# Raw places of the down projection: every second chunk loaded into another tile

## Chip, cores and metric

The kernel runs on one core of a Trainium2 chip. The metric is the device time of one execution in microseconds; the median of some runs is compared. The core has a matmul engine (PE, with its weight loads as PEld), a vector engine (DVE), an activation engine (ACT), GpSimd (POOL), and SyncE (SP), whose queue issues nearly all the transfers here.

## What is computed

A decoder trunk of two layers on 512 rows of 1024 float32 values. Each layer mixes the rows with two kinds of attention heads and then runs a SwiGLU feed-forward network; each half is normed before and after and added to the input:

```python
h = rms_norm(x, attn_pre_g[l])
proj = h @ w_in[l]                 # differential and forgetting heads, both causal
...
x = x + rms_norm(mixed @ w_out[l], attn_post_g[l])

h = rms_norm(x, ffn_pre_g[l])
y = (jax.nn.silu(h @ w_gate[l]) * (h @ w_up[l])) @ w_down[l]
x = x + rms_norm(y, ffn_post_g[l])
```

The hidden width is 2816, so `w_down` is 2816 x 1024. All is float32. Every weight is split into a rounded high part (type float32r) and the remainder, and each product is made of three matmuls: high x high, high x low, low x high.

## The kernel before

**Down projection.** It is done by Strassen's scheme in the Winograd form: seven products of half-size blocks in place of eight. The hidden vectors are kept as "operands" (tiles op00 to op35, a group of six per block or sum, in the pool hp of the layer), the weights as four raw blocks of `w_down` and four sums of blocks, which `weight_sums` (L1215) forms while the gate and up products run and writes to a DRAM scratch `t_d`. Sums of operands are written to `s_d` and come back through `reload` (L1319).

**Chunks.** `product` (L1313) walks over a block's 11 row tiles in six chunks, five of 256 rows and one of 128. For each chunk `chunk_w` (L1298) calls `load_w` (L247): SP loads the raw chunk, 512 KB, into a raw tile; ACT casts it to the high part wh (L258); DVE subtracts to get the low part wl (L259); then 12 matmuls (6 for the short one) use wh and wl. The raw tile has the tag wr with two buffers; wh and wl have three buffers each. The same three tags serve the gate and up weights and the projections of the attention, in program order. There are 42 chunks in a layer, in seven products in the order of L1334 to L1375: banks A_, C_, A_, B_, A_, B_, A_. The last three chunks of the last product are loaded by one statement (`ws`, L1375), and their matmuls are done for one row block after the other, with the post-norm and the next layer's pre-norm between.

**Other tiles that the change touches.** `gain` (L234) loads a row of norm gains, spread over all partitions, into a tile of the pool gpool with the tag gain and two buffers, and pins the load behind what was traced on SP before it. g_apost and g_fpre are used up before the gate and up products; g_fpost and g_apre (of the next layer) are loaded after the last gate and up product. g_fpost is first read at L1356, g_apre in the pre-norm of the next layer. p5, y0, u3 and y2 (L1349) are partial results that take over the tiles op30 to op33 once product 3, which reads group 3, has used them. VA_TAGS (L39) names the operand tiles that serve as raw, high and low tiles for the value weights of the next layer, which are loaded during the last products.

**Order.** Instructions of one engine run in the order in which the framework's scheduler has put them; a tile is given to its next user when all readers of the former one are done, in program order within a tag. In the down projection only the tail after the `ws` loads is pinned by hand.

Of the kernel before, what the change touches and what calls it, by code (L numbers as in the profile page):

```python
# [11 lines left out]
F32 = mybir.dt.float32  # L12
# [5 lines left out]
P = 128  # L18
S = 512
NT = S // P  # L20
D = 1024
# [3 lines left out]
DEPTH = 2  # L25
# [10 lines left out]
TB = S // 16  # L36
VA_C, VA_T = 4, 1
TAIL = 3
VA_TAGS = (("34", "00", "01"), ("34", "02", "03"), ("14", "10", "11"), ("34", "12", "13"))  # L39
KSPLIT = 4  # L40
EPS = 1e-6
BIG = 1e30
# [132 lines left out]
def hymba_block(ctx, tc, x_d, pos_d, apre_d, win_d, fb_d, lq1_d, lk1_d, lq2_d, lk2_d, dsg_d, wout_d, apost_d,  # L175
# [7 lines left out]
    gpool = ctx.enter_context(tc.tile_pool(name="gpool", bufs=2))  # L183
# [50 lines left out]
    def gain(src, l, name):  # L234
        t = gpool.tile([P, D], F32, name=name, tag="gain")
        tc.keep_in_program_order(nc.sync.dma_start(t, src[l].partition_broadcast(P)))
        return t
# [9 lines left out]
    def load_w(src, shape, name, eng=None, dst=None, raw=None):  # L247
        n = int(np.prod(shape[1:]))

        def t(tag, dt):  # L250
            w = wpool.tile([P, WCH], dt, name=f"{tag}_{name}", tag=tag)[:, :n]
            return w.rearrange("p (a b) -> p a b", a=shape[1])
        if raw is None:
            w = wpool.tile([P, WCH], F32, name=f"wr_{name}", tag="wr", bufs=NRAW)[:, :n]
            raw = w.rearrange("p (a b) -> p a b", a=shape[1])
        hi, lo = dst or (t("wh", F32R), t("wl", F32R))
        nc.sync.dma_start(raw, src)
        A.copy(hi, raw)  # L258
        (eng or V).tensor_sub(lo, raw, hi.bitcast(F32))  # L259
        return hi, lo  # L260
# [86 lines left out]
    for l in range(DEPTH):  # L347
# [849 lines left out]
        with ExitStack() as fctx:  # L1197
            hp = fctx.enter_context(tc.tile_pool(name=f"ffn{l}", bufs=1, reuse_waits="tile"))
# [37 lines left out]
            def swiglu(f, pg, pu):  # L1236
                sg = half_tile(f"sg{l}{f}")
                A.activation(sg, pg, AF.Silu)
                V.tensor_mul(sg, pu, sg)  # L1239
                if f < FH:  # L1240
                    first[f] = sg
                    put(0, f, sg[:, :TH])
                    return
                f -= FH
                a11, a21, a12, a22 = (x[:, c] for x in (first.pop(f), sg) for c in (slice(0, TH), slice(TH, S)))
                put(1, f, a12)
                nc.sync.dma_start(s_d[2, f], a22)
                w = half_tile(f"s12{l}{f}")
                s1, s2 = w[:, :TH], w[:, TH:]
                V.tensor_add(s1, a21, a22)  # L1250
                V.tensor_sub(s2, s1, a11)
                put(3, f, s1)
                put(2, f, s2)
                w = half_tile(f"s34{l}{f}")
                s3, s4 = w[:, :TH], w[:, TH:]
                V.tensor_sub(s3, a11, a21)
                V.tensor_sub(s4, a12, s2)
                nc.sync.dma_start(s_d[0:2, f].rearrange("x p n -> p x n"), w.rearrange("p (x n) -> p x n", x=2))
                weight_sums(f)
# [22 lines left out]
            for f in ORDER[2:]:  # L1282
# [1 line left out]
                g_part()  # L1284
                u_part()
                swiglu(f, pg, pu)
            g_fpost = gain(fpost_d, l, f"g_fpost{l}")
            if l + 1 < DEPTH:
                g_apre = gain(apre_d, l + 1, f"g_apre{l + 1}")

            def side(x):

                if x < 4:
                    return t_d[x]
                z, c = divmod(x - 4, 2)
                return wd[z * FH * P:(z + 1) * FH * P, CH[c]]

            def chunk_w(x, q, dst=None):  # L1298
                n = min(2, FH - 2 * q)
                src = side(x)[2 * q * P:(2 * q + n) * P].rearrange("(k p) n -> p k n", p=P)  # L1300
                return load_w(src, [P, n, S], f"d{l}{x}{q}", dst=dst)

            def product_mm(bank, g, q, w, m):
                a = opd[g, q]
                tk = slice(m * P, (m + 1) * P)
                n = a.shape[1]
                for k in range(n):
                    s, e = q == k == 0, q == QN - 1 and k == n - 1
                    mm(bank, a[:, k, 0, tk], w[0][:, k], s, False)
                    mm(bank, a[:, k, 0, tk], w[1][:, k], False, False)  # L1310
                    mm(bank, a[:, k, 1, tk], w[0][:, k], False, e)

            def product(banks, g, x, qs=None):  # L1313
                for q in qs or range(QN):
                    w = chunk_w(x, q)
                    for m in range(2):
                        product_mm(banks[m], g, q, w, m)
# [11 lines left out]
            QN = (FH + 1) // 2  # L1329
            A_, C_, B_ = ([mk(f"d{x}{l}{m}") for m in range(2)] for x, mk in (("a", bank_t), ("c", bank_s),  # L1330
                                                                             ("b", bank_g)))
            name = f"fp{l}"
# [12 lines left out]
            for m in range(2):  # L1345
                V.tensor_add(u[m], A_[m], u[m])
            reload(1, 1)
            product(B_, 3, 0)
            p5, y, u3, y2 = (hp.tile([P, 2, S], F32, name=f"{x}{l}", tag=f"op3{q}") for q, x in enumerate(  # L1349
                ("p5", "y0", "u3", "y2")))  # L1350
            for m in range(2):
                A.copy(p5[:, m], B_[m])
            reload(2, 2)
            for t in range(2):
                ys[t] = y[:, t]
                V.tensor_mul(ys[t], c11[t], g_fpost[:, CH[0]])  # L1356
            product(A_, 0, 2)
            for m in range(2):
                V.tensor_add(u3[:, m], A_[m], u[m])
                V.tensor_add(u[m], p5[:, m], u[m])  # L1360
# [8 lines left out]
            for m in range(2):  # L1369
# [3 lines left out]
                V.tensor_mul(ys[2 + m], ys[2 + m], g_fpost[:, CH[1]])  # L1373
            product(A_, 2, 3, range(QN - TAIL))
            ws = [chunk_w(3, q) for q in range(QN - TAIL, QN)]  # L1375
            if not last:
                for c in range(4):
                    raw, hi, lo = (hp.tile([P, 2, S], dt, name=f"wv{x}{l}{c}", tag=f"op{tag}") for x, dt, tag in zip(
                        "rhl", (F32, F32R, F32R), VA_TAGS[c]))
                    src = win_d[l + 1][2 * c * P:(2 * c + 2) * P, VA:VA + S].rearrange("(k p) n -> p k n", p=P)  # L1380
# [5 lines left out]
            a = f"a{l + 1}"  # L1386
# [43 lines left out]
```

## Time and profile before

| | us |
|---|---|
| median of 3 runs | 1303.62 (1300.08 to 1303.75) |
| profiled execution, in all | 1306.31 |
| its span, first to last instruction | 1304.5 |
| PE busy | 1227.0 (94%) |
| DVE busy | 818.3 (63%) |
| ACT busy | 600.7 (46%) |
| mean granted PE clock | 0.977 |

The span is a little shorter than the execution's time, and the profiled execution is 2.7 us above the median. A busy PE is not a PE at its peak: a matmul of 512 columns shows about 0.39 us of busy time, though the next one starts sooner. So starts, not durations, tell its pace. The granted clock says what share of full speed the chip allowed the matmul engine in a stretch.

### The profile page before, as it was taken

The page shows a single profiled execution, that of the slowest core. Times are in us where ns is not written, and L with a number is a line of the kernel's source. Part 1 is how long each engine was busy: PE and PEld are TensorE (multiplying, and loading weights), DVE is VectorE, ACT ScalarE, POOL GpSimd, SP SyncE. Part 2 cuts the span into 40 slices and gives each one's busy share as a digit, 9 for nine tenths or more (in the row PEclk, how much of TensorE's full clock was granted, in tenths as well). Part 3 has the DMA queues.
Part 4 walks back from the last instruction along what each step waited for, and adds up shares of the span by engine and source line. Part 5 has one row for each costly group of instructions (what it writes and reads, how often), then busy time and mean ns, then how long its engine had stood idle before and what let it go on. Part 6 is the DMA issues. An engine that isn't in the chain of part 4 may idle for free.

```text
span 1304.5 us, 16741 instructions
## 1 busy us (share of the span) xinstructions
PE 1227.0 (94%) x5817; PEld 998.2 (77%) x5817; DVE 818.3 (63%) x1574; ACT 600.7 (46%) x1162; POOL 209.9 (16%) x250
## 2 busy tenths in 40 slices
PE   8999999999999999898899999989999999998885
PEld 6787877898888888666677778768988888876664
DVE  6697768655464646555739876885555555546555
ACT  5476767443332323443535766764423232325432
POOL 1212457210000000000222224761000000000001
PEclk8999999999999999898999999999999999999997
DMA  7233343317676766776413333441366666667543
GB/s 236 75 95 90 89 131 114 96 50 237 202 224 199 222 202 225 255 223 189 144 34 97 98 98 96 117 143 49 107 208 212 212 213 211 217 227 245 184 151 121
DMA packets 211268, 206.75 MB, mean 158 GB/s; under 512 B 11680, under 2 KB 155680, under 8 KB 211184
## 3 DMA queue, kind: packets, MB, share of 16 engines
q1 hardware_dynamic: 211040, 205.16, 51.1%
q8 instruction: 46, 0.75, 0.2%
q10 hardware_dynamic: 144, 0.52, 0.1%
q14 instruction: 38, 0.31, 0.1%
HBM read 163.34 MB, written 33.91 MB: 151 GB/s over the span
## 4 chain that ended last, share of the span: by engine, by line
PE 42%; issue 34%; DVE 15%; ACT 5%; DMA 3%; POOL 2%; POOLq 0%; DVEq 0%; ACTq 0%; SPq 0%
PE pj_g L205 9%; PE pj_u L205 9%; PE o L205 4%; PE va L205 3%; PE pj_kf L205 2%; DMA wr_d<-in_w_down_dram 2%; PE pj_kd L205 2%; PE db L205 1%; PE dc L205 1%; PE pj_qf L205 1%; PE vb L205 1%; DVE ed L958 1%; DVE ed L875 1%; DVE t2kd L739 1%; PE of L205 1%
## 5 line engine op out<-in xcount | busy, mean ns | idle before, releaser
L259 DVE TENSOR_TENSOR wl_d<-wr_d,wh_d 128x1024 fp32r<-128x1024 f32 x84 | 94.3, 1134 | 97.5 <-ACT wh_d L258 96.8
L258 ACT CAST wh_d<-wr_d 128x1024 fp32r<-128x1024 f32 x84 | 81.9, 977 | 148.4 <-DMA wr_d<-t_d 70.1
L205 PE MATMUL pj_g<-hT_h,wh_g 128*128 128x512 f32 (+1 forms) x384 | 142.9, 372 | 0.0
L205 PE MATMUL pj_g<-hT_h,wl_g 128*128 128x512 f32 (+1 forms) x384 | 142.6, 371 | 0.0
L205 PE MATMUL pj_g<-hT_l,wh_g 128*128 128x512 f32 (+1 forms) x384 | 142.6, 371 | 0.0
L205 PE MATMUL pj_u<-hT_h,wh_u 128*128 128x512 f32 (+1 forms) x368 | 140.1, 381 | 0.0
L205 PE MATMUL pj_u<-hT_l,wh_u 128*128 128x512 f32 (+1 forms) x368 | 139.8, 380 | 0.0
L205 PE MATMUL pj_u<-hT_h,wl_u 128*128 128x512 f32 (+1 forms) x368 | 139.7, 380 | 0.0
L271 POOL TENSOR_SCALAR v_fp<-s_fp 128x1 f32<-128x1 f32 x8 | 4.5, 559 | 741.1 <-ACT junk L277 387.2
L205 PE MATMUL da<-wh_d,op 128*128 128x512 f32 x352 | 116.1, 405 | 6.7 <-ACT wh_d L258 6.7
L258 ACT CAST wh_g<-wr_g 128x1024 fp32r<-128x1024 f32 x44 | 46.3, 1053 | 148.0 <-PE pj_u L205 79.2
L259 DVE TENSOR_TENSOR wl_u<-wr_u,wh_u 128x1024 fp32r<-128x1024 f32 x44 | 53.9, 1225 | 96.0 <-ACT wh_u L258 96.0
L258 ACT CAST wh_u<-wr_u 128x1024 fp32r<-128x1024 f32 x44 | 46.3, 1052 | 132.9 <-PE pj_g L205 125.9
L205 PE MATMUL da<-wl_d,op 128*128 128x512 f32 x176 | 73.8, 419 | 19.9 <-DVE wl_d L259 19.6
L205 PEld LDWEIGHTS da<-wh_d,op 128*128 128x128 f32 x352 | 68.3, 195 | 24.5 <-ACT wh_d L258 10.9
L205 PEld LDWEIGHTS pj_g<-hT_h,wh_g 128*128 128x128 f32 x384 | 72.4, 189 | 12.6
L205 PEld LDWEIGHTS pj_g<-hT_l,wh_g 128*128 128x128 f32 x384 | 72.3, 188 | 12.5
L205 PEld LDWEIGHTS pj_g<-hT_h,wl_g 128*128 128x128 f32 x384 | 72.2, 188 | 12.5
L1239 DVE TENSOR_TENSOR sg<-pj_u,sg 128x512 f32<-128x512 f32 x44 | 30.4, 690 | 81.8 <-PE pj_u L205 81.8
L205 PEld LDWEIGHTS pj_u<-hT_l,wh_u 128*128 128x128 f32 x368 | 69.2, 188 | 13.2
L205 PEld LDWEIGHTS pj_u<-hT_h,wl_u 128*128 128x128 f32 x368 | 69.2, 188 | 13.0
L205 PEld LDWEIGHTS pj_u<-hT_h,wh_u 128*128 128x128 f32 x368 | 69.1, 188 | 13.0
(299 smaller groups left out, 2958.1 us busy)
## 6 DMA issues: line engine op xcount, KB each, us to landing
wr_g<-in_w_gate_dram SPq DMA_DIRECT2D x44, 512.0 KB, 4.3
wr_u<-in_w_up_dram SPq DMA_DIRECT2D x44, 512.0 KB, 4.1
b<-in_w_down_dram SPq DMA_DIRECT2D x88, 256.0 KB, 3.4
t_d<-b SPq DMA_DIRECT2D x88, 256.0 KB, 4.1
wr_d<-t_d SPq DMA_DIRECT2D x40, 512.0 KB, 3.8
wr_d<-in_w_down_dram SPq DMA_DIRECT2D x30, 512.0 KB, 4.5
wr_o<-in_w_out_dram SPq DMA_DIRECT2D x16, 512.0 KB, 3.8
rs<-s_d SPq DMA_DIRECT2D x30, 256.0 KB, 5.4
```

The costliest lines, as they stand in the source:

```text
L205: ins = PE.matmul(out, a, b, start=start, stop=stop)
L258: A.copy(hi, raw)
L259: (eng or V).tensor_sub(lo, raw, hi.bitcast(F32))
L271: G.tensor_scalar(v, s2[:, 0:1], scalar1=s2[:, 1:2], scalar2=EPS, op0=ALU.add, op1=ALU.add)
L739: return V.tensor_mul(b["t2"], b["t2"], sinT)
L875: return V.tensor_tensor_reduce(out=b["e"][:, :n], in0=b["s"][:, :n], in1=addend, scale=-0.125, scalar=3.0e38, op0=ALU.add, op1=ALU.min, a ...
L958: return V.scalar_tensor_tensor(e0, e0, b["r"][:, 0:1], e1, op0=ALU.mult, op1=ALU.add)
L1239: V.tensor_mul(sg, pu, sg)
```

## The change

Every second raw chunk of the down projection is no longer loaded into a wr tile. A counter over the chunks of a layer picks the place: even chunks keep wr; odd ones of the first four products take a tile of gpool (tag gain), odd ones of the last three products take op32 or op33 in turn. So that these tiles are free, the two gain rows g_fpost and g_apre are loaded after product 3 is traced, u3 and y2 move to op00 and op01 and are allocated after product 4 (the one on A_ with weight block 2), and the value weights of the next layer get other operand tiles.

```diff
-VA_TAGS = (("34", "00", "01"), ("34", "02", "03"), ("14", "10", "11"), ("34", "12", "13"))
+VA_TAGS = (("34", "02", "03"), ("34", "04", "10"), ("30", "11", "12"), ("34", "13", "14"))
...
-            g_fpost = gain(fpost_d, l, f"g_fpost{l}")
-            if l + 1 < DEPTH:
-                g_apre = gain(apre_d, l + 1, f"g_apre{l + 1}")
...
+            chunks = itertools.count()
+
             def chunk_w(x, q, dst=None):
                 n = min(2, FH - 2 * q)
                 src = side(x)[2 * q * P:(2 * q + n) * P].rearrange("(k p) n -> p k n", p=P)
-                return load_w(src, [P, n, S], f"d{l}{x}{q}", dst=dst)
+                z = next(chunks)
+                raw = None
+                if z % 2:
+                    if z < 4 * QN:
+                        raw = gpool.tile([P, D], F32, name=f"xr{l}{x}{q}", tag="gain")
+                    else:
+                        raw = hp.tile([P, 2 * S], F32, name=f"xr{l}{x}{q}", tag=("op32", "op33")[z // 2 % 2])
+                    raw = raw[:, :n * S].rearrange("p (a b) -> p a b", a=n)
+                return load_w(src, [P, n, S], f"d{l}{x}{q}", dst=dst, raw=raw)
...
             product(B_, 3, 0)
-            p5, y, u3, y2 = (hp.tile([P, 2, S], F32, name=f"{x}{l}", tag=f"op3{q}") for q, x in enumerate(
-                ("p5", "y0", "u3", "y2")))
+            p5, y = (hp.tile([P, 2, S], F32, name=f"{x}{l}", tag=f"op3{q}") for q, x in enumerate(("p5", "y0")))
+            g_fpost = gain(fpost_d, l, f"g_fpost{l}")
+            if l + 1 < DEPTH:
+                g_apre = gain(apre_d, l + 1, f"g_apre{l + 1}")
...
             product(A_, 0, 2)
+            u3, y2 = (hp.tile([P, 2, S], F32, name=f"{x}{l}", tag=f"op0{q}") for q, x in enumerate(("u3", "y2")))
```

## Rows read from the trace of the kernel before

**Rows 1.** The page's 40 equal slices of the span, PE busy in tenths.

```profile
PE   8999999999999999898899999989999999998885
```

**Rows 2.** Windows: start:end and length, then each engine's busy us, PEclk, DMA share, GB/s.

```profile
510.67:588.24 77.57, 67.15 (x265) 51.51 (x264) 43.91 (x59) 35.94 (x52) 0.00 (x0) 0.93 0.75 240
588.24:628.25 40.01, 35.04 (x132) 26.29 (x133) 22.01 (x24) 15.17 (x17) 0.00 (x0) 0.91 0.58 182
628.25:651.98 23.73, 18.60 (x75) 14.07 (x75) 18.36 (x24) 13.76 (x28) 7.65 (x10) 0.93 0.47 140
1154.44:1233.76 79.32, 67.68 (x265) 50.41 (x264) 44.34 (x59) 35.82 (x52) 0.00 (x0) 0.96 0.69 226
1233.76:1271.24 37.48, 33.06 (x133) 25.35 (x133) 18.69 (x21) 12.11 (x14) 0.00 (x0) 0.95 0.49 154
1271.24:1296.64 25.40, 18.31 (x66) 14.06 (x66) 13.83 (x18) 8.06 (x15) 3.46 (x6) 0.80 0.35 114
```

**Rows 3.** Timeline of PE, start of product 0, layer 0: start us, length, instruction.

```profile
511.58 0.39 PE L205 MATMUL da<-wl_d,op 128*128 128x512 f32 x1
...
512.26 0.39 PE L205 MATMUL da<-wl_d,op 128*128 128x512 f32 x1
```

**Rows 4.** Waits of the whole span: waiter, releaser, us in total, times, longest.

```profile
ACT wh_d L258 <- DMA wr_d<-t_d: 70.1, 35, 7.7
...
ACT wh_d L258 <- DMA wr_d<-in_w_down_dram: 49.6, 26, 7.1
```

**Rows 5.** Waits of SP's own queue, 510.67 to 628 us.

```profile
SPq L257 <- DVE wl_d L259: 59.4, 29, 4.7
```

**Rows 6.** Timeline of DVE, then of ACT, product 4 of layer 1.

```profile
1233.74 1.23 DVE L259 TENSOR_TENSOR wl_d<-wr_d,wh_d 128x1024 fp32r<-128x1024 f32 x1 [4.40 <-ACT wh_d L258]
...
1239.72 1.23 DVE L259 TENSOR_TENSOR wl_d<-wr_d,wh_d 128x1024 fp32r<-128x1024 f32 x1 [3.33 <-ACT wh_d L258]
...
1245.88 1.22 DVE L259 TENSOR_TENSOR wl_d<-wr_d,wh_d 128x1024 fp32r<-128x1024 f32 x1 [2.80 <-ACT wh_d L258]
...
1244.80 1.05 ACT L258 CAST wh_d<-wr_d 128x1024 fp32r<-128x1024 f32 x1 [2.97 <-DMA wr_d<-t_d]
```

**Rows 7.** Timelines of SP, ACT and PE around the end of product 0, layer 0.

```profile
521.41 0.74 SPq L236 DMA_DIRECT2D g_fpost<-in_ffn_post_g_dram  x1
...
523.24 1.42 SPq L257 DMA_DIRECT2D wr_d<-in_w_down_dram  x2
...
530.07 1.04 ACT L258 CAST wh_d<-wr_d 128x1024 fp32r<-128x1024 f32 x1 [1.98 <-DMA wr_d<-in_w_down_dram]
...
531.17 1.22 PE L205 MATMUL dc<-wh_d,op 128*128 128x512 f32 x2 [3.76 <-ACT wh_d L258]
```

**Rows 8.** Window of product 2, layer 0, columns as in rows 2.

```profile
549.20:569.17 19.97, 16.31 (x67) 11.87 (x65) 14.65 (x21) 13.12 (x21) 0.00 (x0) 1.00 0.88 287
```

**Rows 9.** Timelines of DVE and PE in product 2 and at product 5's start, layer 0.

```profile
548.72 1.37 DVE L1342 TENSOR_TENSOR c<-dc,u 128x512 f32<-128x512 f32 x2 [3.53 <-PE dc L205]
...
551.28 0.50 PE L205 MATMUL da<-wl_d,op 128*128 128x512 f32 x1 [1.46 <-DVE wl_d L259]
...
605.59 1.37 DVE L1359 TENSOR_TENSOR u<-da,u 128x512 f32<-128x512 f32 x2 [1.37 <-PE da L205]
606.88 1.28 DVE L1360 TENSOR_TENSOR u<-p,u 128x512 f32<-128x512 f32 x2
```

**Rows 10.** Timelines of DVE and PE in product 6, layer 1.

```profile
1269.76 1.37 DVE L1364 TENSOR_TENSOR u<-db,u 128x512 f32<-128x512 f32 x2 [2.89 <-PE db L205]
...
1277.58 2.35 DVE L259 TENSOR_TENSOR wl_d<-wr_d,wh_d 128x1024 fp32r<-128x1024 f32 x2
...
1278.85 0.79 PE L205 MATMUL da<-wl_d,op 128*128 128x512 f32 x1 [6.88 <-DVE wl_d L259]
```

**Rows 11.** Timeline of SP, loads ahead of the gate and up products, layer 0.

```profile
226.13 0.42 SPq L236 DMA_DIRECT2D g_fpre<-in_ffn_pre_g_dram  x1
230.09 0.38 SPq L257 DMA_DIRECT2D wr_g<-in_w_gate_dram  x1
```

## Prediction

> **What bounds the kernel now.** I read the slices of the span first: the matmul engine is busy in nine tenths or more of nearly every slice, and of the nine slices under that, seven lie in two places, three between 522 and 652 us and the last four, from 1174 us to the end [rows 1]. These are the down projections of the two layers, seven products of 66 matmuls each, and the change touches nothing else. So second I took the busy time of each engine by product groups there [rows 2]. I number the seven products p0 to p6 and the chunks z = 0 to 41, six to a product, the sixth of half size. In layer 0, p0 to p3 take 77.57 us, p4 and p5 40.01 us, p6 23.73 us; in layer 1 79.32, 37.48 and 25.40 us.
>
> What would they take if nothing were late? In a stretch without waits every third matmul starts 0.68 us after the last such one, so 0.2267 us each [rows 3]; a whole chunk (12 matmuls) is 2.72 us and a product (66) 14.96 us. Four products are 59.84 us, two 29.92 us. The excess is then 17.73 + 10.09 + 8.77 us in layer 0 and 19.48 + 7.56 + 10.44 us in layer 1, together 74.1 us. This is all that the change can win; part of it is waits and part is the clock, granted at 0.80 to 0.96 of full speed over these groups, which means that the engine spent some of the time at 1.2 GHz instead of 2.4 GHz [rows 2].
>
> Third, what ends the waits. Over the whole kernel the cast of a chunk (L258) sat idle 70.1 us and 49.6 us until a load of the raw chunk had landed [rows 4], and between the starts of p0 and p6 the loads themselves were held 59.4 us in layer 0 until a subtraction (L259) had let go of a raw place [rows 5]. So the chain is load, cast, subtract, next load, and two places carry it. One turn of a place can be read in p4 of layer 1, where little else moves: the subtractions of every second chunk end at 1234.97, 1240.95 and 1247.10, and in the last turn the load lands for a cast at 1244.80 [rows 6]. A turn is 6.0 to 6.15 us, 3.0 us a chunk with two places, against 2.72 us of matmuls. That is the lightest case. At the end of p0 of layer 0 two loads issued from 523.24 on are cast only from 530.07 on, and the matmuls wait 3.76 us [rows 7]; there a turn is about 9 us, 4.5 us a chunk. The raw places set the pace in both.
>
> **The change part by part.** *Four places instead of two.* Even chunks stay in the two wr tiles, odd ones go to two gain tiles up to z = 23 and to op32 and op33 from z = 25. A place is now needed again after four chunks. By the 6.0 to 9 us turn that is 1.5 to 2.3 us a chunk, under the 2.72 us of matmuls, so the places no longer set the pace. Next late is the wh tile of the cast, of which there are three: cast z waits for the matmuls of z - 3, and 2.72 + 2.72 us of matmuls lie between, or 4.08 us where the half chunk is among them, against 1.05 + 1.23 us of cast and subtraction [rows 6]. That is 1.8 to 3.2 us of slack, so the matmuls set the pace except where a queue holds a cast or a subtraction longer. No instruction is added: the same 84 loads, casts and subtractions.
>
> *Transfers.* p0 to p3 move 77.57 us x 240 GB/s = 18.6 MB and 79.32 us x 226 GB/s = 17.9 MB, and the same bytes must come in a shorter time. The most that a product moved is 287 GB/s, at a DMA share of 0.88 [rows 8]. At that rate p0 to p3 take 64.9 and 62.5 us, 5.1 and 2.7 us over the 59.84 us. I take these 7.8 us. The lower end is 0 (at share 1.0 the rate would be 326 GB/s, and 18.6 MB would take 57 us), the upper end no gain at all there, the first rival. The Trainium skill, DMA: Bandwidth & Descriptors, section "Where 436 GB/s comes from", has about 358 GB/s of HBM as what binds a load from HBM; by it 18.6 MB would be an estimated 52 us, the 7.8 us would drop out, and the time would be 1254 us. No stretch of this trace reaches it.
>
> *Order on ACT and DVE.* Casts and subtractions stand in line with the reload of the operands and with the additions out of the banks. In p2 two additions of 1.37 us stand ahead of a subtraction and the matmuls wait 1.46 us [rows 9]. Such a collision stays when the load is early. Bounds are 0 (it fits in the slack of 1.8 to 3.2 us) and 2 us (that row, with some clock) for each of the 12 products p0 to p5; with 1 us it is 12 us, the middle, because the slack is as long as most of these runs. At the start of p5 two pairs of additions, 1.37 + 1.28 us, stand ahead of a subtraction [rows 9], more than the short slack of 1.8 us: I leave another 1.9 us in p4 and p5 of each layer, 3.8 us.
>
> *p6.* In layer 1 the subtraction of z = 36 stands on DVE behind the post-norm of the first two row blocks, which runs from 1269.76 to 1277.58, and the matmuls wait 6.88 us and go on at the low clock [rows 10]. With four places z = 36 and 37 are cast as the matmuls of z = 33 and 34 end, before that run begins; the first that can meet it is z = 38, needed 5.44 us after the last product ends. If it stands behind the whole run of 7.8 us, its own 1.23 us bring it 3.6 us late; if it slips into a wait for POOL, nothing. I leave 4 us of the 10.44. In layer 0 DVE is busy 18.36 us in p6 [rows 2]; two subtractions leave it and one of the next layer's weights is pushed into it, so 18.36 - 1.23 = 17.1 us against 14.96 us of matmuls: at least 2.2 us remain, at most the 8.77 us of now; I take 5.
>
> *The gain loads.* g_fpost and g_apre leave the end of p0, where they stand in SP's queue right ahead of the late loads of z = 6 and 7 [rows 7], and come behind the load of z = 23, after the raw chunks of z = 21 and z = 23 let go of their places. They are pinned behind it, so on SP the loads of z = 24 on and the reloads are what can be queued behind them; z = 24's place is free about 2.4 us into p3, before g_fpost's, so it can pass. If it doesn't, z = 24 is about 3 us late, once in a layer, inside the 2 us a product of above and its neighbour's slack. The two products with g_fpost (L1356) only feed the post-norm three products later: nothing. The first two odd chunks can be loaded as soon as g_apost and g_fpre are free, at the start of the gate and up products: 1 MB, 3.7 us at 287 GB/s, beside loads that lead by three wh tiles: nothing, and at most 3.7 us a layer.
>
> *p5's and the value weights' tiles.* u3 and y2 go to op00 and op01, which product 4 has just read; u3 waits for that product anyhow. The value weights of the next layer get other tiles, free only as chunks of p4 and p5 are used up; one split lands in p6 and is counted above.
>
> **The sum.** Left over: 7.8 + 12 + 3.8 + 4 + 5 = 32.6 us of 74.1. The gain is 41.5 us. The profiled execution is 1304.5 us of span and 1306.3 us in all, so it would be 1264.8 us; the median of the runs is 2.7 us under it, 1303.6, and the forecast 1303.6 - 41.5 = 1262.1 us. With the ends of the terms, left over 2.2 + 3.8 = 6 us would give 1235.5 us; with 24 us of collisions, 7.8, 3.8 and an unchanged p6 (19.2) left over is 54.8 us and the time 1284.3 us. I call 1243 to 1285 us the forecast's own range; its low end is drawn in because all terms would have to be at their least together.
>
> **Rivals.** *Transfers or the queues bind p0 to p3.* For it: a DMA share of 0.88 in p2 and 0.75 over p0 to p3 of layer 0, and loads that take 6.8 us [rows 2, 7, 8]. Against: its share over p4 and p5 is 0.58 and 0.49, and the loads gain some four chunks of lead, 10.9 us, over the 6.8 us. If p0 to p3 keep their time and only p4 to p6 win (17.65 - 3.8 - 4 and 19.2 - 9), the gain is 20 us: 1283.5 us. Chance 0.2.
>
> *The loads come no earlier.* SP issues in order, and a load that waits for its place holds all behind it. If odd and even loads are lined up so that each waits for the one before, the odd place is free but its load isn't issued: no change, about 1303 us. Against: loads wait for a subtraction, not for each other [rows 5]. Chance 0.05.
>
> *Slower: early casts take the wh tiles.* The odd chunks z = 1 and 3 can be loaded 200 us before their matmuls. If their casts are then put ahead of the gate and up weights' casts, they hold two of the three wh tiles all that time. One taken tile costs nothing (2.28 us of cast and subtraction beside 24 x 0.2267 = 5.44 us of matmuls); it decides from the second on: with one tile each of some 40 gate and up products in a layer waits about 2.3 us, 184 us in all: 1488 us. Against: in the kernel before nothing was pulled ahead of earlier users of its tag; the first gate weight, which waits for nothing but a wr tile, is loaded only at 230.09, after the pinned gains [rows 11]. Chance 0.06.
>
> **How the numbers follow.** Forecast 0.69, rivals 0.2, 0.05 and 0.06. The range 1243 to 1285 us takes in the forecast but for its ends and most of the first rival. Faster by over 0.3% (about what a measurement of this kernel can tell): forecast and first rival, 0.89; within 0.3%: 0.05; slower: 0.06.
>
> **What would show it.** Right: casts of chunks that wait for matmuls instead of loads, products p1 to p5 of 15 to 17 us, granted clock near 1.00 in them, p6 of layer 1 at 18 to 20 us, DMA near 290 GB/s in p0 to p2. Wrong: casts that still wait over 40 us for loads in each layer (first two rivals), p0 to p3 over 70 us with a DMA share of 0.9 (transfers), waits in the gate and up products (early casts).

## Result and profile after

| | before | after |
|---|---|---|
| median, us | 1302.66 (1300.08 to 1303.75, 4 runs) | 1250.46 (1247.25 to 1252.08, 4 runs) |
| ratio | | 0.9599 (95% interval 0.9574 to 0.9624) |
| profiled execution, its span | 1306.31, 1304.5 | 1249.71, 1247.9 |
| mean granted PE clock | 0.977 | 0.993 |

The kernel is 4.0% faster, 52.2 us by the medians. The two profiled executions differ by 56.6 us, since that of before lay 3.7 us above its median and that of after 0.8 us below.

The page of after, the same 40 slices as in [rows 1]: PE busy in tenths.

```profile
PE   8999999999999999999799999999999999999996
```

Nine slices were under nine tenths; now three are: the first, the one from 593 to 624 us, where p5 of layer 0 ends and most of its p6 runs, and the last, with p6 of layer 1.

The windows of the same product groups as in [rows 2]: start and end, length, busy us of PE, PEld, DVE, ACT and POOL, granted clock, DMA share, GB/s.

```profile
512.70:572.53 59.83, 59.83 (x265) 49.56 (x264) 45.00 (x59) 35.46 (x51) 0.00 (x0) 1.00 0.91 295
572.53:605.22 32.69, 30.53 (x134) 24.70 (x132) 19.51 (x21) 15.60 (x18) 0.00 (x0) 1.00 0.82 269
605.22:630.46 25.24, 18.94 (x75) 14.17 (x74) 20.32 (x27) 13.90 (x30) 7.44 (x10) 0.93 0.26 78
1128.79:1189.72 60.93, 60.16 (x265) 49.48 (x264) 44.78 (x59) 34.61 (x50) 0.00 (x0) 1.00 0.88 295
1189.72:1221.63 31.91, 30.46 (x133) 24.70 (x132) 17.45 (x19) 13.60 (x15) 0.00 (x0) 1.00 0.60 189
1221.63:1239.98 18.35, 15.27 (x67) 12.12 (x65) 13.20 (x18) 7.08 (x14) 3.85 (x6) 1.00 0.28 98
```

Read the lengths against [rows 2], group by group. p0 to p3 fell from 77.57 to 59.83 us and from 79.32 to 60.93 us; in layer 0 PE has no idle time left in them. p4 and p5 fell from 40.01 to 32.69 and from 37.48 to 31.91 us. p6 fell from 25.40 to 18.35 us in layer 1 but **rose** from 23.73 to 25.24 us in layer 0. Together 283.51 us became 228.95: 54.6 of the 56.6 us of the two profiles. The other 2.0 us lie outside the products, as differences of 2 to 4 us of either sign in the attention and around it; no run here takes them apart. The granted clock is 1.00 in all groups but one.

The casts and subtractions of the chunks: what the engine waited for ahead of them, in us and times.

```profile
  ACT wh_d L258: 50.1, 37
  PE da L205: 38.0, 26
  PE db L205: 12.1, 8
...
  DMA xr<-t_d: 7.5, 2
  DMA wr_d<-in_w_down_dram: 4.6, 2
```

In [rows 4] the casts waited 119.7 us for loads; now 12.1 us. Instead they wait 50.1 us until matmuls let go of a wh tile (38.0 us for matmuls into da, 12.1 us for those into db): the cast is ahead of the matmuls, and matmuls set the pace. The first line is another wait that happens to be as long in all, that of a subtraction for its cast.

Per product, from PE start to PE start (14.96 us is the pace of matmuls alone): layer 0 has 14.96 in p0 to p3 and p5, 17.72 in p4 and 25.24 in p6; layer 1 has 14.96 in p0, p2, p3 and p5, 16.05 in p1, 16.95 in p4 and 18.35 in p6. So 19.5 us are left over in five places, and the experiments went for the reason of the gain first and for these five after it.

### The profile page after: what moved, and what is told of

It reads as the page before. It is cut to its first block, busy times and chain, and to the rows that moved or that the text cites. A ratio compares the mean times of both kernels' runs of the same rounds, so it can differ in the third digit from the quotient of the medians.

```text
span 1247.9 us, 16724 instructions
## 1 busy us (share of the span) xinstructions
PE 1201.7 (96%) x5817; PEld 989.3 (79%) x5817; DVE 817.3 (65%) x1574; ACT 599.2 (48%) x1162; POOL 210.4 (17%) x250
## 4 chain that ended last, share of the span: by engine, by line
PE 44%; issue 32%; DVE 13%; ACT 4%; DMA 4%; POOL 2%; SPq 0%; POOLq 0%; DVEq 0%; ACTq 0%
PE pj_g L205 10%; PE pj_u L205 10%; PE o L205 4%; PE va L205 3%; PE pj_kf L205 2%; PE pj_kd L205 2%; PE da L205 2%; PE pj_qf L205 2%; DMA rs<-s_d 2%; PE vb L205 1%; DVE t2kd L739 1%; PE db L205 1%; PE ptf L210 1%; DVE ed L958 1%; PE of L205 1%
## 5 line engine op out<-in xcount | busy, mean ns | idle before, releaser
L205 PE MATMUL da<-wh_d,op 128*128 128x512 f32 x352 | 111.3, 392 | 2.1 <-ACT wh_d L258 2.1
L205 PE MATMUL da<-wl_d,op 128*128 128x512 f32 x176 | 69.7, 396 | 10.9 <-DVE wl_d L259 10.9
L205 PEld LDWEIGHTS pj_u<-hT_h,wh_u 128*128 128x128 f32 x368 | 69.2, 188 | 13.1
L258 ACT CAST wh_d<-wr_d 128x1024 fp32r<-128x1024 f32 x42 | 44.2, 1052 | 42.4 <-PE da L205 15.4
L259 DVE TENSOR_TENSOR wl_d<-wr_d,wh_d 128x1024 fp32r<-128x1024 f32 x42 | 51.3, 1222 | 19.2 <-ACT wh_d L258 18.6
```

The lines of the kernel that those rows point to most:

```text
L205: ins = PE.matmul(out, a, b, start=start, stop=stop)
```

## Experiments

Ratios are to the kernel before, run beside each experiment on the same chip. Its median was 1299.25 us beside the two-place run, the first three-place build and the single edits for p4 and p6, 1302.57 and 1302.31 us beside the others, and 1302.66 us beside the changed kernel; so a difference in us to the changed kernel's median can be some 3 us off, and the product lengths of the profiles are read beside it. The diffs are against the changed kernel. An expectation calls the theories by letters: A is that the number of raw places set the pace, D that one late chunk makes p4's loss, F that DVE's order makes p6's.

### Two places, the rest of the change kept

```diff
-                if z % 2:
+                if False:
```

> The changed kernel with one thing undone: every chunk is again loaded into the two wr tiles; the later gain loads, u3 and y2 in op00 and op01 and the other tiles of the value weights stay. Theory A (the number of raw places set the pace): the two places bind again at 3.0 to 4.5 us a chunk, products p1 to p5 take 18 to 21 us each, and the time is 1292 to 1303 us; the up to 10 us under the kernel before are what the gain loads give that no longer stand before z = 6 and 7. Rival B (the moved gain loads and tiles did it, the places hide nothing): products of about 15 us and 1250 to 1262 us. Between the two, 1270 to 1285 us, each would have a share.

Measured: 1300.94 us (1296.71 to 1306.09), ratio 1.0007 (0.9984 to 1.0031). With everything moved but the places, nothing is gained, and the products take 18 to 20 us again up to p5. The longest waits for loads, of the whole span, stand as they did in [rows 4]:

```profile
ACT wh_d L258 <- DMA wr_d<-t_d: 72.8, 33, 7.6
ACT wh_d L258 <- DMA wr_d<-in_w_down_dram: 51.9, 22, 6.9
```

The whole gain comes from the places. The moved gain loads, the other tiles of u3 and y2 and those of the value weights are worth nothing by themselves; they only make the places free.

### Three places, in two builds

In the first, g_fpost stays where the kernel before loads it, so that only one gain tile is left for raw chunks; every third chunk goes there, and from z = 24 on to op32.

```diff
+            g_fpost = gain(fpost_d, l, f"g_fpost{l}")
...
-                if z % 2:
+                if z % 3 == 2:
...
-                        raw = hp.tile([P, 2 * S], F32, name=f"xr{l}{x}{q}", tag=("op32", "op33")[z // 2 % 2])
+                        raw = hp.tile([P, 2 * S], F32, name=f"xr{l}{x}{q}", tag="op32")
...
-            g_fpost = gain(fpost_d, l, f"g_fpost{l}")
             if l + 1 < DEPTH:
                 g_apre = gain(apre_d, l + 1, f"g_apre{l + 1}")
```

> The changed kernel with three raw places in rotation: every third chunk goes to one gain tile (from z = 24 on to op32), the others to the two wr tiles; g_fpost is loaded after the last gate and up product as in the kernel before and holds the other gain tile, g_apre after p3. Theory A (places, with a turn of 6.0 us where little moves and about 9 us where much does): 2.0 to 3.0 us a chunk against 2.72 us of matmuls, so p3 to p5 at 15 to 16 us as with four places, p0 to p2 up to 2 us longer each: 1251 to 1264 us. Rival C (the lead over busy transfers counts, not the turn: each place gives the same): half of the gain, 1272 to 1282 us.

Measured: 1271.15 us (1269.93 to 1280.19), ratio 0.9783 (0.9741 to 0.9826). The total alone misleads: p0 takes 29.89 and 29.83 us, and p1 to p3 14.96, 14.96 and 15.15 us in layer 0 and 14.96 each in layer 1. SP issues the load of the third chunk only behind the pinned load of g_fpost:

```profile
519.97 0.44 SPq L236 DMA_DIRECT2D g_fpost<-in_ffn_post_g_dram  x1
520.46 8.40 SPq L257 DMA_DIRECT2D xr<-in_w_down_dram  x2
```

This is over 10 us after p0's start at 509.68, and the casts of such chunks waited 27.1 us in three waits, up to 13.7 us. It is a stall of this edit, once a layer, and no price of three places. The second build keeps the gain rows where the changed kernel has them and lets one tile of the gain pool take every third chunk:

```diff
-                if z % 2:
+                if z % 3 == 2:
                     if z < 4 * QN:
-                        raw = gpool.tile([P, D], F32, name=f"xr{l}{x}{q}", tag="gain")
+                        xr1 or xr1.append(gpool.tile([P, D], F32, name=f"xr{l}", tag="gain"))
+                        raw = xr1[0]
...
-                        raw = hp.tile([P, 2 * S], F32, name=f"xr{l}{x}{q}", tag=("op32", "op33")[z // 2 % 2])
+                        raw = hp.tile([P, 2 * S], F32, name=f"xr{l}{x}{q}", tag="op32")
```

> Three raw places from the first chunk on without the stall that e2_three_places had at its third chunk: one tile of the gain pool a layer takes every third chunk (z mod 3 = 2, below 24), op32 does from 24 on, the gain rows stay where the changed kernel has them. Theory A (a chunk's place turns round in 6 to 9 us while a chunk of matmuls lasts 2.72 us, so three places of some 8 us in all are enough): products 0 to 5 at 14.96 but for the known one at product 4, the time within 1245 to 1256, nearly that of four places. Rival B (each further place gives about the same, so three give half): 1272 to 1282, products 0 to 3 near 16.9.

Measured: 1250.11 us (1247.64 to 1252.06), ratio 0.9598 (0.9567 to 0.9628): the time of four places. So the places give no equal share each. Two are too few, three are about enough, as the turn of 6 to 9 us against chunks of 2.72 us has it. Not quite enough: p2 and p3 of layer 0 take 15.63 and 16.76 us and p3 of layer 1 15.80, and p0 to p5 together 95.0 and 92.9 us against 92.5 and 92.8 with four places. All seven products of both layers are 2.2 us longer than with four in the profiles, which the medians (1250.11 and 1250.46) don't show.

### The late chunk of p4

SP around p4's start in the changed kernel, layer 0, then what ACT and PE waited for:

```profile
565.36 0.35 SPq L236 DMA_DIRECT2D g_fpost<-in_ffn_post_g_dram  x1
565.80 0.38 SPq L1331 DMA_DIRECT2D rs<-s_d  x1
567.70 0.37 SPq L257 DMA_DIRECT2D wr_d<-t_d  x1
568.91 0.33 SPq L236 DMA_DIRECT2D g_apre<-in_attn_pre_g_dram  x1
569.29 0.94 SPq L257 DMA_DIRECT2D xr<-t_d  x2
...
575.71 1.04 ACT L258 CAST wh_d<-xr 128x1024 fp32r<-128x1024 f32 x1 [3.07 <-DMA xr<-t_d]
...
576.81 0.49 PE L205 MATMUL da<-wh_d,op 128*128 128x512 f32 x1 [1.39 <-ACT wh_d L258]
```

z = 25 is the first chunk for op32, whose last reader in p3, the matmuls of z = 20, ended at 565.74. Its load is issued at 569.29, 3.5 us later: ahead of it on SP stand the load of z = 26 (567.70), which waits for the wr tile of z = 22, and then g_apre (568.91), which waits for the gain tile of z = 23. It lands for a cast at 575.71. Layer 1 is the last and loads no g_apre, and yet its p4 loses 1.99 us:

```profile
1184.17 0.37 SPq L257 DMA_DIRECT2D wr_d<-t_d  x1
1184.63 1.94 SPq L257 DMA_DIRECT2D xr<-t_d  x2
...
1192.19 1.05 ACT L258 CAST wh_d<-xr 128x1024 fp32r<-128x1024 f32 x1 [4.43 <-DMA xr<-t_d]
```

There op32 is free at 1182.92, and only the load of z = 26 (1184.17) stands between. So g_apre is a part of the delay, in layer 0. The first three-place build points the same way: its p4 takes 16.58 us in layer 0 and 14.96 us in layer 1. The edit leaves the raw chunks in the gain tiles through z = 29 and moves the gain rows and y's two products with g_fpost behind p4:

```diff
-                    if z < 4 * QN:
+                    if z < 5 * QN:
...
-            g_fpost = gain(fpost_d, l, f"g_fpost{l}")
-            if l + 1 < DEPTH:
-                g_apre = gain(apre_d, l + 1, f"g_apre{l + 1}")
             for m in range(2):
                 A.copy(p5[:, m], B_[m])
             reload(2, 2)
-            for t in range(2):
-                ys[t] = y[:, t]
-                V.tensor_mul(ys[t], c11[t], g_fpost[:, CH[0]])
             product(A_, 0, 2)
+            g_fpost = gain(fpost_d, l, f"g_fpost{l}")
+            if l + 1 < DEPTH:
+                g_apre = gain(apre_d, l + 1, f"g_apre{l + 1}")
+            for t in range(2):
+                ys[t] = y[:, t]
+                V.tensor_mul(ys[t], c11[t], g_fpost[:, CH[0]])
```

> The changed kernel with the two gain rows loaded after product p4 instead of p3, the odd chunks of p4 still in gain tiles, op32 and op33 used from z = 31 on. It asks where the waits at z = 25 come from, 2.76 us in layer 0 and 1.99 us in layer 1. Theory D (the load of z = 25 is issued late, since its place op32 is free only after the matmuls of z = 20 and the pinned gain load stands before it on SP): p4 takes 14.96 us in both layers and the time falls by 4 to 5 us, to about 1246 us. Rival E (the transfers are saturated around the start of p4, whichever is loaded): the waits stay or move to the next chunks, and the time stays within 1.5 us of 1250.5 us.

Measured: 1242.41 us (1241.03 to 1245.19), ratio 0.9544 (0.9512 to 0.9576). Windows of p0 to p5 and p6, layers 0 and 1:

```profile
512.77:602.53 89.76, 89.76 (x397) 74.32 (x396) 65.35 (x80) 51.63 (x69) 0.00 (x0) 1.00 0.89 295
602.53:627.06 24.53, 18.81 (x75) 14.16 (x74) 19.57 (x27) 13.16 (x29) 7.48 (x11) 0.93 0.28 79
1124.60:1214.36 89.76, 89.76 (x397) 74.33 (x396) 62.29 (x78) 48.34 (x65) 0.00 (x0) 1.00 0.82 267
1214.36:1235.46 21.10, 18.02 (x67) 14.13 (x65) 13.19 (x18) 7.08 (x14) 3.87 (x6) 0.84 0.23 85
```

Six products in 6 x 14.96 = 89.76 us, in both layers, without any idle time of PE. p4's loss was the late load. Which part of the edit it took is not shown: z = 25 now goes to the tile of z = 21 and is issued in layer 0 at 564.06, ahead of the load of z = 26 at 566.67, and the gain rows are out of the way as well. In layer 1, p6 grew from 18.35 to 21.10 us and took back most of the 3.1 us won ahead of it. The products are 3.8 us shorter in the profile and its span 4.5; the medians differ by 8.0, since this profiled execution (1245.19) lay 2.8 us above its median and that of the changed kernel 0.8 us below.

### The last product's chunks ahead of the norm

DVE and PE in p6 of the changed kernel, layer 0 (compare [rows 10]):

```profile
615.37 1.42 DVE L286 SCALAR_TENSOR_TENSOR h_a<-xs,r_a,g_apre 128x512 f32<-128x512 f32 x2 [0.76 <-POOL r_a L272]
616.71 0.68 DVE L313 TENSOR_TENSOR y_fp<-u,g_fpost 128x512 f32<-128x512 f32 x1
617.31 0.74 DVE L316 SCALAR_TENSOR_TENSOR xs<-y,r_fp,xs 128x512 f32<-128x512 f32 x1
617.97 0.74 DVE L316 SCALAR_TENSOR_TENSOR xs<-y_fp,r_fp,xs 128x512 f32<-128x512 f32 x1
618.63 1.21 DVE L259 TENSOR_TENSOR wl_d<-wr_d,wh_d 128x1024 fp32r<-128x1024 f32 x1
...
619.90 0.50 PE L205 MATMUL da<-wl_d,op 128*128 128x512 f32 x1 [2.01 <-DVE wl_d L259]
...
623.97 0.50 PE L205 MATMUL da<-wl_d,op 128*128 128x512 f32 x1 [2.42 <-DVE wl_d L259]
```

The subtraction of z = 40 stands behind norm work, and PE waits for it. Five such waits, 0.52 to 2.42 us, make 6.3 us. The edit gives the loads, casts and subtractions of the last product's chunks a higher priority in the scheduler, so that they go ahead of the norm's work where both are ready:

```diff
-                return load_w(src, [P, n, S], f"d{l}{x}{q}", dst=dst, raw=raw)
+                with tc.high_priority(1000) if z >= 6 * QN else nullcontext():
+                    return load_w(src, [P, n, S], f"d{l}{x}{q}", dst=dst, raw=raw)
```

> The changed kernel with the loads, casts and subtractions of the last product's six chunks given priority in the scheduler's order, so that on DVE the subtractions of z = 37 to 41 come ahead of most of the post-norm and pre-norm of the first two row blocks. It asks what p6 still loses, 10.3 us in layer 0 and 3.4 us in layer 1. Theory F (the order on DVE: subtractions stand behind norm work that is not urgent): p6 takes 15 to 17 us in layer 1 and 16 to 20 us in layer 0, and the time falls by 4 to 8 us, to 1243 to 1247 us. Rival G (the amount of DVE work binds, about 17 to 20 us in layer 0, and what is put off comes back before the next layer's transposes): p6 gets shorter but the norms end later by as much, and only layer 1's 2 to 3 us are won: 1247 to 1249 us, or nothing.

Measured: 1237.68 us (1235.09 to 1242.23), ratio 0.9515 (0.9482 to 0.9548). Windows of p6, layers 0 and 1:

```profile
602.04:618.77 16.73, 16.22 (x75) 13.06 (x74) 13.89 (x19) 10.38 (x23) 4.43 (x8) 1.00 0.41 114
1213.12:1228.08 14.96, 14.96 (x67) 12.20 (x65) 12.99 (x18) 7.08 (x14) 4.82 (x6) 1.00 0.34 119
```

p6 fell from 25.24 to 16.73 and from 18.35 to 14.96 us, with no instruction removed, and the clock stays at 1.00. In layer 0 the DVE work within p6 is 13.89 us instead of 20.32: 27 instructions became 19, and the others now run after the product's end. They are not free there. From p6's end to the first projection of the next layer, in the changed kernel and then here:

```profile
630.46:656.08 25.62, 25.29 (x121) 20.36 (x120) 10.58 (x17) 10.14 (x19) 7.34 (x8) 1.00 0.05 13
618.77:649.00 30.23, 27.31 (x121) 21.49 (x120) 15.87 (x26) 12.80 (x25) 8.52 (x10) 0.94 0.04 10
```

PE now waits 2.7 us there for subtractions of the norm (hT_l), at a granted clock of 0.94: of the 8.5 us that p6 of layer 0 won, 4.6 come back. So theory F holds for p6 itself, and rival G for over half of what it wins in layer 0; layer 1, with no layer behind it, keeps its 3.4 us. That makes 7.3 of the 11.8 us between the two spans. p1, p3 and p4, which the edit doesn't touch, are 2.7 us shorter in all, and the rest lies outside the products.

### Both edits

The two diffs above together.

> Both edits of the two runs before it: the raw chunks lie in the gain pool's tiles through chunk 29 and the gain rows are loaded after product 4, and the loads, casts and subtractions of the last product's chunks go ahead of the norm's work. If the two losses are independent (theories D and F), the 3.2 us that e4_p6_first still had in products 3 and 4 (1.87 + 1.02 + 0.29) go and nothing else changes: 1237.7 - 3.2 = 1234.5, between 1231 and 1238, products 0 to 5 at 14.96 in both layers. Rival: gain rows that land later push the norm run later into product 6 (in e3 product 6 of layer 1 grew from 18.35 to 21.10, 2.75 us); if that can't be hidden by the order of the last chunks either, 1237 to 1241.

Measured: 1233.23 us (1231.21 to 1236.56), ratio 0.9469 (0.9446 to 0.9493), 17.2 us under the changed kernel's median. Windows of p0 to p5 and p6:

```profile
509.69:599.45 89.76, 89.76 (x397) 74.33 (x396) 65.31 (x81) 51.69 (x69) 0.00 (x0) 1.00 0.89 296
599.45:616.12 16.67, 16.19 (x76) 13.10 (x74) 13.82 (x19) 10.33 (x23) 4.43 (x8) 1.00 0.40 111
1116.71:1206.47 89.76, 89.76 (x397) 74.35 (x396) 62.46 (x78) 48.45 (x65) 0.00 (x0) 1.00 0.82 267
1206.47:1221.43 14.96, 14.96 (x67) 12.20 (x65) 12.99 (x18) 7.09 (x14) 4.83 (x6) 1.00 0.33 119
```

Layer 1 takes 104.72 us, seven times 14.96; layer 0 has 1.7 us more in p6, where the window also holds eight transposes of the next layer's norm (1.0 us) and a wait of 0.48 us. The down projection is at the pace of its matmuls, and this is the best version here. The stretch behind p6 of layer 0 stays as long as in the run before:

```profile
616.12:646.40 30.28, 26.14 (x121) 20.21 (x120) 15.89 (x26) 12.57 (x25) 8.53 (x10) 1.00 0.04 10
```

So the rival, that late gain rows push the norm run further, did not come, but the norm run is waited for behind p6 (PE 3.4 us for hT_l in products of the next layer). In the profiles the products are 17.8 us shorter than in the changed kernel, 4.7 us come back in this stretch, and the other 5.4 of the 18.5 us between the spans lie elsewhere and are not taken apart.

### How near the transfers are to their bound

The prediction left 7.8 us to the transfers, and p0 to p3 of layer 0 show none. Was there room, or was it close? Four runs add 18 transfers a layer that nobody waits for, one for each reloaded operand. In the first two they are copies from DRAM to DRAM on SP's queue, of 128 KB and of 256 KB:

```diff
                     nc.sync.dma_start(raw, s_d[s, 2 * q:2 * q + n].rearrange("k p n -> p k n"))
+                    tc.keep_in_program_order(nc.sync.dma_start(x_d2[s, q], wd[q * P:q * P + P // 2, CH[0]]))
```

> The changed kernel and, behind each of the 18 reload loads a layer, one more transfer of 128 KB from DRAM to DRAM on the same queue that nobody waits for: 0.79 MB more in each of the products 1 to 3 or so, 4.41 + 0.79 = 5.20 MB in 14.96 us, 347 GB/s, where the changed kernel moved 295 to 305. Theory T0 (the transfers have room): products 1 to 3 stay within 0.3 us of 14.96, the time within 3 us of the changed kernel's 1250.5. Theory T1 (they are at their bound near 326 GB/s, which is 295 over its busy share of 0.91): 5.20 MB / 326 = 15.9 us, 1 us more in each of six products, 1254 to 1259. Theory T2 (297 to 305 GB/s is the most there is): 5.20 / 0.305 = 17.0 us, 2.1 us more in each, 1260 to 1266.

> The same with 256 KB in each added transfer: 4.41 + 1.57 = 5.98 MB in a product, 400 GB/s if it should last 14.96 us. T0 (room beyond 400): 1250 to 1254. T1 (326 GB/s): 18.3 us a product, 3.4 us more in each of six, 1268 to 1274. T2 (305 GB/s): 19.6 us, 4.6 more in each, 1276 to 1282. How the product lengths of the two runs stand to 14.96 gives the rate at which transfers begin to set the pace.

Measured: 1269.11 us (1260.52 to 1269.44), ratio 0.9727 (0.9692 to 0.9762) with 128 KB, and 1276.5 us (1272.62 to 1280.1), ratio 0.9799 (0.9768 to 0.983) with 256 KB. 18.6 and 26.0 us more than the changed kernel: more than the expectation for a bound at 305 GB/s in the first, inside it in the second. But the first product with the additions (p1, layer 0) moves 322 GB/s and is only 0.36 us longer than 14.96, while the longest one (p3, 22.92 us) moves 262, so a plain rate explains neither. Twice the bytes cost only 1.4 times as much, so something else costs too. Two more runs parted slots and bytes: 2 KB copies at the same places in SP's queue, and 256 KB writes of the reloaded operand on GpSimd's queue, which is idle here; with them the order on SP, ACT and DVE from p0 to p4 stays that of the changed kernel.

```diff
+                    tc.keep_in_program_order(nc.sync.dma_start(x_d2[s, q], wd[q * P:q * P + 1, CH[0]]))
```

> The changed kernel with the 18 added transfers a layer on SyncE's queue at the same places as in e8_more_transfers, but of 2 KB each: the slots in the queue without the bytes. Theory S (the queue): most of what e9 and e8 lost, 1261 to 1275. Theory T (the bytes): within 3 us of 1250.5. If cost is a + b x bytes through e9 (18.6 us at 128 KB) and e8 (26.0 at 256 KB), the part of the slots is 11.2 us: 1262.

```diff
                     V.tensor_sub(x[:, :, 1], raw, x[:, :, 0].bitcast(F32))
+                    nc.gpsimd.dma_start(x_d2[s, q], x[:, 0].rearrange("p a b -> p (a b)"))
```

> The changed kernel and, after each reloaded operand, a 256 KB write of that operand from the chip's memory to DRAM, issued on GpSimd's queue (idle in this stage) and waited for by nobody: 1.57 MB more in each of three products a layer, the bytes of e8_more_transfers without its slots in SyncE's queue. If the bytes were what cost e8 its 26 us (theory T: 4.41 + 1.57 = 5.98 MB at the 350 GB/s that e8 reached at a busy share of 1.00 is 17.1 us, 2.1 more in each of six products), about 1263, at least 1260. If SyncE's queue was (theory S: six loads of 0.6 us more ahead of the weight loads of each product), 1250 to 1254, products 1 to 3 within 0.3 us of the changed kernel's.

Measured: slots alone 1261.86 us (1260.63 to 1264.94), ratio 0.969 (0.9664 to 0.9715); bytes alone 1261.2 us (1260.97 to 1262.91), ratio 0.9691 (0.9669 to 0.9712). Each costs about 11 us; neither theory holds alone. The expectation of the slots run, a fixed part of 11.2 us and a price by bytes (1262 us), came true. The three runs with copies on SP's queue have one and the same order on SP, ACT and DVE, so between them only the bytes differ: 7.2 us more for 128 KB than for 2 KB, 14.6 us more for 256 KB. Windows of p1 to p4, layer 0, bytes alone:

```profile
524.91:539.87 14.96, 14.96 (x67) 12.39 (x66) 10.57 (x13) 9.72 (x14) 3.45 (x6) 1.00 1.03 356
539.87:554.83 14.96, 14.96 (x67) 12.39 (x66) 10.22 (x14) 9.29 (x15) 3.20 (x6) 1.00 1.08 349
554.83:574.87 20.04, 17.46 (x68) 13.37 (x67) 13.32 (x17) 9.36 (x13) 3.20 (x6) 0.91 1.09 364
574.87:595.22 20.35, 16.95 (x68) 13.37 (x66) 8.35 (x8) 8.26 (x10) 0.00 (x0) 0.92 0.76 250
```

At 349 to 356 GB/s p1 and p2 lose nothing; p3 at 364 loses 5.1 us, and p4, with nothing added, takes 20.35, 2.6 us more than in the changed kernel. In layer 1 p2 takes 15.26 us at 327 GB/s and p3 21.12 us at 351, so no one rate divides the products that lose from those that don't. The casts of reloaded operands wait for their loads, 15.1 us over p1 to p4 up to 3.8 us at a time (9.0 us in the changed kernel), and the chunk casts stand behind them on ACT. That the lead of the loads pays for two products and is used up in the third is an inference; no run varies it. Windows of p2 to p4, layer 0, slots alone:

```profile
541.50:559.59 18.09, 15.46 (x67) 12.12 (x65) 12.36 (x17) 10.19 (x16) 0.00 (x0) 1.00 0.66 217
559.59:582.78 23.19, 17.17 (x67) 13.36 (x67) 11.46 (x15) 9.93 (x14) 0.00 (x0) 0.91 0.76 258
...
582.78:601.00 18.22, 18.18 (x67) 14.28 (x67) 9.64 (x9) 7.88 (x8) 0.00 (x0) 0.83 0.69 212
```

Here the DMA share is 0.66 to 0.76 and yet p3 takes 23.19 us. SP's order is what changed, and that on ACT and DVE with it: the reloads and copies of a product are now issued in one block, ahead of weight loads of the next product and in p3 partly behind g_fpost and g_apre. Whether the slots or this order costs the 11 us these runs don't part, since pinning the copies moved the reloads among the weight loads too. The p4 row shows a second price: PE is busy 18.18 of 18.22 us, so it hardly waits, but at a granted clock of 0.83, so part of the time at 1.2 instead of 2.4 GHz, after 6 us without work in p3. 3.3 us are lost without a wait of their own, and p5 is back at 14.96 us and 1.00.

## Why the prediction was right, and where its sizes were off

The mechanism was right: 1262.1 us with 1243 to 1285 was predicted, and 1250.46 came. Two places set the pace, four take it off the path, and next late is the wh tile: the casts do wait for PE (50.1 us), and the two-place run shows that nothing else in the change gains. The rivals fell. p0 to p3 didn't keep their time; the loads came earlier; and although z = 1 and z = 3 are loaded from 273.83 us on, at the start of gate and up, their casts were not pulled ahead (the first cast of a chunk outside wr begins at 507.28, just before p0).

The forecast was 11.6 us too high against the median. Against the profiled execution, on which the sum was made (41.5 us of gain, 56.6 measured), it is 15.1 us: 13.1 in the terms below and the 2.0 us outside the products. Left over, in us:

| term | predicted | measured |
|---|---|---|
| transfers, p0 to p3 | 7.8 | 1.1, by another cause |
| collisions on ACT and DVE, p0 to p5 | 12 | 0 seen |
| more of them in p4 and p5 | 3.8 | 4.7, by another cause |
| p6, layer 1 | 4 | 3.4 |
| p6, layer 0 | 5 | 10.3 |
| sum | 32.6 | 19.5 |

**Collisions: 12 us too much.** Of the bounds of 0 and 2 us a product the lower was the value. No product from p0 to p5 that was late was late by additions ahead of a subtraction. The slack of 1.8 to 3.2 us that the prediction had worked out is enough for one run of 1.37 us, and the order itself changed. At p2's and p5's start, where two additions stood together in [rows 9], a subtraction now stands between the first two: the scheduler has a chunk ready for it by then. That the earlier casts are why it puts them so was not tried by itself. The edit that fixed p4 shows it best: without any late load, six products in both layers have no idle time at all.

**Transfers: 6.7 us too much.** The 287 GB/s of [rows 8] was the rate of a product that stalled on other things, not a bound. p1 of the changed kernel, layer 0:

```profile
527.65:542.62 14.97, 14.97 (x68) 12.39 (x67) 10.58 (x13) 9.66 (x14) 0.00 (x0) 1.00 0.99 325
```

The other value weighed, 326 GB/s at share 1.0, is what happens: share 0.99 at 325 GB/s, and PE waits for nothing. The Trainium skill, DMA: Bandwidth & Descriptors, section "Where 436 GB/s comes from", has about 358 GB/s of HBM as the bound of loads from it. No run here moves loads alone at that rate; with a quarter of the bytes writes, 349 to 364 GB/s were moved, near its figure and in one product above it. The 1.1 us is the load of z = 8 in p1 of layer 1, for which its cast waited 3.38 us. It was late by SP's queue and not by the rate: its wr tile was free at 1136.79, when the subtraction of z = 4 ended, and the load was issued 4.9 us later, behind the last writes of the weight sums:

```profile
1135.56 1.23 DVE L259 TENSOR_TENSOR wl_d<-wr_d,wh_d 128x1024 fp32r<-128x1024 f32 x1 [0.47 <-ACT wh_d L258]
...
1140.04 1.52 SPq L1226 DMA_DIRECT2D t_d<-b  x3
1141.68 0.41 SPq L257 DMA_DIRECT2D wr_d<-in_w_down_dram  x1
```

So the rival with chance 0.2 was wrong at this demand, but the added bytes and slots show how near it was: a third more bytes in three products cost 10.7 us.

**p4: right in size, wrong in cause.** I had put 3.8 us on additions at p5's start; p5 lost nothing and p4 lost 2.76 and 1.99 us, to the late load of z = 25. The part on the gain loads saw the queue and priced it at about 3 us once a layer, but for z = 24, and took it as hidden in its neighbours' slack. z = 24 came in time, issued 3.1 us into p3. What was not asked is when op32 comes free, which is after matmuls and not after a subtraction, and what stands ahead of z = 25 on SP: the load of z = 26 in both layers, and g_apre in layer 0.

**p6.** Layer 1 came as worked out, 3.4 us for 4: z = 38 stands behind the norm run and PE waits 3.08 us once. In layer 0 the term was 5.3 us short. I took DVE's work there for the bound (17.1 us). The waits are those of order, five for subtractions that stand behind norm work, and the window held 20.32 us of DVE work, three instructions more than before, two of them additions of p5's result. The run with the last chunks first shows that p6 need not hold this work: it takes 16.73 us with 13.89 us of it. But the norm work does count for the layer, since 4.6 us came back behind p6.

The two errors had opposite signs, 18.7 us too much in the first two terms and 5.3 too little in p6 of layer 0. That p4 came near its 3.8 us was luck. The range held because its lower end was drawn towards the case that these terms vanish.

## What to carry over

Count the places of a load, cast and subtract chain by its turn over the pace of its user: 6 to 9 us over 2.72 us said three to four, and three gave the time of four while two gave nothing. Once the stall is off the path, price what remains by which instruction stands in front of which on an in-order engine or queue: late loads on SP's queue and a few subtractions behind norm work cost the products 17.8 us, a third of what the change won in them, with no work removed. Then look behind the product too: 4.6 us came back there, where the norm work that had been put off was waited for. A rate read in a stretch that waits on something else is a floor, not a bound.

## What the hardware showed that was not expected

Transfers can fill the DMA engines without any price for PE: 325 GB/s at share 0.99, and 349 to 356 GB/s for two products, went beside matmuls at full pace; the price came in the third. And a stall can be paid twice: in the run with slots alone, after 6 us of idle time in one product, the next ran at a granted clock of 0.83 (1.2 GHz for part of it) with almost no waits and took 18.22 us instead of 14.96. The kernel before shows the same in p1 of layer 0, after a p0 with 4.8 us of idle time:

```profile
531.17:549.20 18.03, 17.99 (x67) 14.16 (x67) 10.62 (x13) 8.97 (x12) 0.00 (x0) 0.84 0.71 224
```

So a part of what the places won there is clock and no wait: PE was busy 17.99 of 18.03 us before, and the product takes 14.96 us now.
